# A table of offsets to the planner's order in a gated DeltaNet layer: heads' stages, out-projection operands and feed-forward groups

## The chip, the cores and the metric

The kernel runs on one core of one Trainium2 chip. The metric is device time in microseconds (us) of one execution; the median of three executions is compared. The core has a matrix engine (TensorE, "PE" in the profile, with its weight loads as "PEld"), a vector engine (VectorE, "DVE"), a scalar engine (ScalarE, "ACT"), GpSimd ("POOL") and a queue that issues DMAs (SyncE, "SP"). Each engine takes its own instructions strictly in the order in which the program holds them, and waits for the others through semaphores.

## The reference, cut to what matters

One layer (`DEPTH = 1`, so the gated DeltaNet mixer alone), 2048 tokens, width 1024: one input projection, eight heads of chunked linear attention and four heads of attention over a memory of 256 rows side by side, one output projection, a norm, a squared-ReLU feed-forward of width 4096, a norm.

```python
def gdn_mixer(x, mem_k, mem_v, w_in, conv_w, a_log, dt_bias, gate_norm_w, w_out):
    proj = x @ w_in                                   # q, k, v, z of 8 heads, gates a and b, queries to the memory
    qkv = silu(causal_depthwise_conv(proj[..., :3072], conv_w))
    q, k = l2_normalize(heads(q)), l2_normalize(heads(k))
    beta = sigmoid(b); g = -exp(a_log) * softplus(a + dt_bias)
    o = chunk_gated_delta_rule(q, k, v, g, beta)      # a triangular solve per chunk, then a recurrence over chunks
    o = rms_norm(o, gate_norm_w) * silu(heads(z))
    m = memory_attention(mq, mem_k, mem_v)
    return concatenate([o, m], axis=-1) @ w_out

x = layer_norm(ALPHA * x + gdn_mixer(x, ...), ln1_g, ln1_b)
x = layer_norm(ALPHA * x + square(relu(x @ w_ff1)) @ w_ff2, ln2_g, ln2_b)
```

## The kernel before

**Tiling and stages.** The 2048 tokens are four blocks of 512 (`b` = 0 to 3), taken two at a time (`s` = 0, 1). For each pair the program runs the mixer of block 2s, the mixer of block 2s+1, the output projection of both (`out_seven`), the first feed-forward product (`ff1`) and the second (`ff2`). The two blocks of a pair form one 2x2 block matrix product, done in seven products in place of eight, so operands such as A11, S2 or T3 are sums and differences of parts. Every large product is done three times over (`mm3`: high part by high, high by low, low by high), which needs each operand split into two parts: ACT casts the high part, DVE subtracts to get the low part (`split`, `split_in_place`). Weights go through a pool `whl` of four buffers; a weight tile is loaded by SP, cast by ACT and subtracted by DVE before PE may use all of it (its first two of three products need only the cast).

**A mixer** (`mixer(b, ...)`) has steps t = 0 to 9. In step t it records stage B (`gdn_b`, the recurrence of head t-2, and its delivery), stage A (`gdn_a`, decays, inverse of the 64x64 triangles and other preparations of head t-1), stage D (`dense`: the projections q, k, v of head t, whose matmuls write `aq`, `ak`, `av`, with convolution), stage Z (`gate`: the projection `az`), from t = 5 to 8 stage M (one head of attention over the memory: `amq`, `sps`, `pmT`, `pmo`), and in block 0 stage Y (`memory`: the memory's rows, keys `amk` and values `amv`, which are computed once). In block 1 two stages K and O prepare weights for later.

**The recurrence** of one head has four chunks, and each has the same chain across three engines: PE multiplies by the state (`pc<-state,ck`), DVE forms `R`, PE multiplies by the inverse (`pc<-R,Y`), ACT copies to `vt`, PE forms the state's update (`pc<-vt,kd`), DVE adds it to `state`, and the next chunk starts. `po` is the head's output, `pto` its transpose.

**What sets the order.** The functions do not issue anything: a `Recorder` keeps every operation in the order in which the code meets it. `issue()` (L291) then plans: it goes through a model of five engines with a cost for each operation (`cost`, L256) and a latency for each pair of engines, and whenever an engine comes free takes, of the operations that are ready on it, the one with the lowest `prio` (line 210). `prio` is the operation's number in the recording plus `shift`, a number set at a few places by hand. The operations are then issued, engine by engine, in the planned order, all from one line (L408), so that the profile tells groups apart by tile alone. Buffers are given out in the order in which the code first names them, whatever the `prio`: an operation that is moved ahead still waits for a buffer until those named before it have theirs.

**The output projection** (`out_seven`, with `part` inside) makes each operand (`operand`: X, from DRAM scratch `xo`) and its weights (`weights`: from `wos` scratch or `w_out`) when it is first needed. `ff1` starts with `second_half`, in which y is transposed (`pt<-ident,y`) and split into the operands `B`. While this goes on, `begin(p)` for p = 0 to 2 gives PE products that need none of it: `fA<-T,we` and `fB<-T,we`, with weights prepared in stage K. Then come 16 groups `rest(p)`.

Of the kernel before, what the change touches and what calls it, by code (L numbers as in the profile page):

```python
# [188 lines left out]

class Recorder:  # L190
    def __init__(self, nc, tc):
        self.nc, self.tc, self.ops, self.shift, self.gate = nc, tc, [], 0, None
# [13 lines left out]
    def add(self, eng, fn, name, args, kw):  # L206
# [3 lines left out]
        o.prio = o.i + self.shift  # L210
# [214 lines left out]
def hybrid_layer(  # L425
# [85 lines left out]
    nc = rec  # L511
    state = [rec.buf(cst, (P, P), F32, "state%d" % h, 1, "state") for h in range(H)]
# [763 lines left out]
    def second_half(ys, T0d, B, between):  # L1276
# [16 lines left out]
        for e2 in range(2):  # L1293
            c = slice(e2 * 2 * P, (e2 + 1) * 2 * P)
            for k in K2:
                if not e2:
# [25 lines left out]
    def ff1(s, ys, T0d, B):  # L1322
# [276 lines left out]
    def mixer(b, T, w0, G):  # L1599
        i = b % 2  # L1600
        r, A, z = {}, {}, {}
        for t in range(H + 2):
            if t >= 2:
                c = cat_tile()
                gdn_b(t - 2, A.pop(t - 2), G, z.pop(t - 2), c[0])
                deliver(i, t - 2, *c)
            if 1 <= t <= H:
                A[t - 1] = gdn_a(t - 1, r.pop(t - 1), G)
            if t < H:
                r[t] = dense(b, t, T, G, None if t else w0)  # L1610
            for n in Z_AT.get(t, ()):
                z[n] = gate(b, n, T)
            if t in MEM_AT:
# [3 lines left out]
                deliver(i, H + h, *c)  # L1617
            if b == 0 and t >= MEMORY:
                memory(t - MEMORY)
            if b == 1 and t in KEEP_FF:  # L1620
# [3 lines left out]
                rec.shift, rec.gate = 0, None  # L1624
            if b == 1 and 1 <= t <= 6:
# [11 lines left out]
    def out_seven(s, x1d, T0d):  # L1637
# [36 lines left out]
        def part(n, t, u, first, last):  # L1674
            xn, wn, bn, outs, on = OUT[n]
            if (n, u) not in xs:
                rec.gate = held.get(GATE.get(n))
                xs[n, u] = operand(n, xn, u)
                ws[n, u] = weights(wn, u)
                rec.gate = None  # L1680
# [35 lines left out]
        def first(t):  # L1716
            standardize(ys[t], x1d[t])
            if t % 2:
                keep_T(ys, T, T0d, t // 2)
# [126 lines left out]
```

## Time and profile before

| | us |
|---|---|
| median of three runs (2736.44 to 2738.46) | 2736.44 |
| the profiled execution's own time | 2735.04 |
| its span, from the first to the last instruction | 2733.3 |
| PE busy within the span | 2710.0 |
| DVE / ACT / POOL busy | 2109.6 / 1636.4 / 403.2 |
| mean granted TensorE clock | 0.999 |

The difference between the execution's time and its span, 1.7 us, lies outside the program's instructions. "Busy" counts the time in which at least one instruction of the engine is in flight. The stages follow each other on PE: both mixers of the first pair to about 655 us, output projection to 770, `ff1` to 1081, `ff2` to 1385, then the same for the second pair: mixers to 2005, projection to 2110, `ff1` to 2419, `ff2` to the end.

### The profile page before, as it was taken

The page shows a single profiled execution, that of the slowest core. Times are in us where ns is not written, and L with a number is a line of the kernel's source. Part 1 is how long each engine was busy: PE and PEld are TensorE (multiplying, and loading weights), DVE is VectorE, ACT ScalarE, POOL GpSimd, SP SyncE. Part 2 cuts the span into 40 slices and gives each one's busy share as a digit, 9 for nine tenths or more (in the row PEclk, how much of TensorE's full clock was granted, in tenths as well). Part 3 has the DMA queues.
Part 4 walks back from the last instruction along what each step waited for, and adds up shares of the span by engine and source line. Part 5 has one row for each costly group of instructions (what it writes and reads, how often), then busy time and mean ns, then how long its engine had stood idle before and what let it go on. Part 6 is the DMA issues. An engine that isn't in the chain of part 4 may idle for free.

```text
span 2733.3 us, 42460 instructions
## 1 busy us (share of the span) xinstructions
PE 2710.0 (99%) x13605; PEld 2267.3 (83%) x13605; DVE 2109.6 (77%) x5644; ACT 1636.4 (60%) x4106; POOL 403.2 (15%) x1030
## 2 busy tenths in 40 slices
PE   9999999999999999999999999999999999999998
PEld 7888888888888888888888888888888888888887
DVE  7899889998877777655778887888878666567575
ACT  7778767676475555334446766677756655553341
POOL 3233223321000000000033321232101000000000
PEclk9999999999999999999999999999999999999999
DMA  8666548876788888766754445444578644476673
GB/s 319 224 228 224 209 168 300 302 257 242 267 311 288 293 279 299 261 212 202 265 209 146 153 146 185 169 137 163 203 274 294 229 160 141 162 275 225 210 240 112
DMA packets 208543, 613.99 MB, mean 225 GB/s; under 512 B 23072, under 2 KB 32192, under 8 KB 188352
## 3 DMA queue, kind: packets, MB, share of 16 engines
q1 hardware_dynamic: 207888, 611.23, 64.2%
q8 instruction: 107, 1.75, 0.3%
q14 instruction: 116, 0.95, 0.1%
q10 hardware_dynamic: 432, 0.05, 0.0%
HBM read 436.54 MB, written 174.65 MB: 224 GB/s over the span
## 4 chain that ended last, share of the span: by engine, by line
PE 92%; DVE 4%; ACT 2%; issue 1%; DMA 1%; POOL 1%; SPq 0%; DVEq 0%; POOLq 0%; ACTq 0%
PE f2A L408 13%; PE fA L408 12%; PE ao L408 8%; PE f2C L408 6%; PE aq L408 6%; PE av L408 6%; PE fC L408 6%; PE az L408 6%; PE ak L408 6%; PE f2B L408 3%; PE pc L408 3%; PE amq L408 3%; PE fB L408 3%; PE po L408 2%; PE pkq L408 2%; PE pq L408 1%
## 5 line engine op out<-in xcount | busy, mean ns | idle before, releaser
L408 DVE TENSOR_TENSOR whl<-wraw,whl 128x512 fp32r<-128x512 f32 (+2 forms) x294 | 257.3, 884 | 111.2 <-ACT whl L408 108.6
L408 ACT CAST whl<-wraw 128x512 fp32r<-128x512 f32 (+2 forms) x294 | 226.6, 780 | 159.9 <-PE fC L408 54.7
L408 PE MATMUL fA<-B,whl 128*128 128x512 f32 x1152 | 276.9, 390 | 0.0
L408 PE MATMUL f2A<-whl,X 128*128 128x512 f32 x1152 | 262.1, 389 | 0.0
L408 ACT CAST X<-X 128x1024 fp32r<-128x1024 f32 x118 | 123.9, 1052 | 219.8 <-DMA X<-xsc 194.8
L408 PEld LDWEIGHTS fA<-B,whl 128*128 128x128 f32 x1152 | 216.1, 188 | 45.2 <-DVE B L408 0.2
L408 PEld LDWEIGHTS f2A<-whl,X 128*128 128x128 f32 x1152 | 216.3, 188 | 44.8
L408 DVE TENSOR_TENSOR X<-X,X 128x1024 fp32r<-128x1024 f32 x118 | 143.9, 1222 | 128.2 <-ACT X L408 128.0
L408 PE MATMUL aq<-T,whl 128*128 128x512 f32 x768 | 219.9, 411 | 5.6 <-ACT T L408 5.6
L408 PE MATMUL ak<-T,whl 128*128 128x512 f32 x768 | 215.3, 408 | 0.0
L408 PE MATMUL az<-T,whl 128*128 128x512 f32 x768 | 210.2, 405 | 0.0
L408 PE MATMUL av<-T,whl 128*128 128x512 f32 x768 | 208.2, 404 | 0.0
L408 PE MATMUL fC<-B,whl 128*128 128x512 f32 x768 | 185.6, 390 | 0.7 <-DVE B L408 0.7
L408 PE MATMUL f2C<-whl,X 128*128 128x512 f32 x768 | 174.7, 389 | 0.0
L408 PEld LDWEIGHTS fC<-B,whl 128*128 128x128 f32 x768 | 144.0, 188 | 31.4 <-DVE B L408 1.6
L408 PEld LDWEIGHTS f2C<-whl,X 128*128 128x128 f32 x768 | 144.2, 188 | 29.9
L408 PEld LDWEIGHTS aq<-T,whl 128*128 128x128 f32 x768 | 137.1, 192 | 27.7 <-ACT T L408 5.6
L408 PEld LDWEIGHTS av<-T,whl 128*128 128x128 f32 x768 | 138.4, 189 | 23.5
L408 PEld LDWEIGHTS ak<-T,whl 128*128 128x128 f32 x768 | 136.6, 189 | 22.3
L408 PEld LDWEIGHTS az<-T,whl 128*128 128x128 f32 x768 | 136.8, 189 | 22.0
L408 POOL TENSOR_SCALAR ve<-mv 128x1 f32<-128x1 f32 x34 | 16.8, 495 | 915.1 <-DVE mv L408 911.4
L408 PE MATMUL ao<-whl,X 128*128 128x512 f32 x528 | 139.8, 403 | 0.1
(294 smaller groups left out, 6272.4 us busy)
## 6 DMA issues: line engine op xcount, KB each, us to landing
whl<-wsc SPq DMA_DIRECT2D x108, 1024.0 KB, 5.0
wraw<-in_w_ff_dram SPq DMA_DIRECT2D x106, 512.0 KB, 4.6
X<-xsc SPq DMA_DIRECT2D x96, 512.0 KB, 3.9
wsc<-whl SPq DMA_DIRECT2D x36, 1024.0 KB, 6.1
whl<-tsc SPq DMA_DIRECT2D x64, 512.0 KB, 4.8
xsc<-hB SPq DMA_DIRECT2D x96, 256.0 KB, 3.1
xo<-cat SPq DMA_DIRECT2D x80, 256.0 KB, 3.9
wraw<-in_w_in_dram SPq DMA_DIRECT2D x35, 512.0 KB, 6.1
```

Source lines behind the costliest of these rows:

```text
L408: o.fn(*[res(a) for a in o.args], **{k: res(v) for k, v in o.kw.items()})
```

## The change

A table `PLACE` gives numbers to some stages. A new function `spot(*key)` looks its key up, and the number found (0 if there is none) is added to the `prio` of every operation recorded until the next call. So 82 places get an offset between -600 and +600: a negative one lets the operations of that stage go ahead of others that are ready, a positive one lets them stand back. No operation is added, removed or altered, and every engine has the same instructions before and after. Keys are (block, step, stage) in the mixers, (s, n, u, "X" or "W") for operand and weights of product n in the output projection, (s, p, "F") for feed-forward groups, (s, t, "n") for the standardization of a row tile after the output projection, and ("w",) for the three early groups.

```diff
+PLACE = {
+    ('w',): 445, (0, 0, 'F'): -65, (0, 1, 'Y'): 285, (0, 2, 'D'): -5, (0, 2, 'Y'): -225, (0, 2, 'n'): 600,
...
+    (1, 5, 0, 'X'): 10, (1, 5, 2, 'W'): -375, (1, 6, 0, 'W'): 15, (1, 6, 2, 'X'): -25,
+}
...
-        o.prio = o.i + self.shift
+        o.prio = o.i + self.shift + self.base
...
+    def spot(*key):
+        rec.base = PLACE.get(key, 0)
...
+        spot("w")
         between()
+        spot(None)
...
         for p in range(NP):
+            spot(s, p, "F")
             rest(p)
+            spot(None)
...
         for t in range(H + 2):
+            spot(b, t, "B")
             if t >= 2:
                 c = cat_tile()
                 gdn_b(t - 2, A.pop(t - 2), G, z.pop(t - 2), c[0])
                 deliver(i, t - 2, *c)
+            spot(b, t, "A")
             if 1 <= t <= H:
                 A[t - 1] = gdn_a(t - 1, r.pop(t - 1), G)
+            spot(b, t, "D")
             if t < H:
                 r[t] = dense(b, t, T, G, None if t else w0)
...
                 rec.gate = held.get(GATE.get(n))
+                spot(s, n, u, "X")
                 xs[n, u] = operand(n, xn, u)
+                spot(s, n, u, "W")
                 ws[n, u] = weights(wn, u)
+                spot(None)
```

The order on the engines, at three places that matter (rows of the built program, L408 before is L424 after).

**PE, block 0, first chunks of head 0's recurrence.** `pc`, `po` belong to the recurrence, `pp`, `pq` to the inverse of head 1, `ptk` to head 2's keys. Before:

```order
L408 MATMUL ptv<-ident,cv 128x128 x4
L408 MATMUL pp<-inv 112x32 x2
L408 MATMUL pc<-R,Y 128x128
L408 MATMUL ptk<-ident,ck 128x128 x4
L408 MATMUL pc<-vt,kd 128x128
L408 MATMUL po<-vt,at 128x128
L408 MATMUL pq<-Lq,inv 128x32 x2
L408 MATMUL pc<-state,ck 128x128
L408 MATMUL po<-state,qd 128x128
L408 MATMUL pp<-inv 128x32 x2
L408 MATMUL pc<-R,Y 128x128
L408 MATMUL pc<-vt,kd 128x128
```

After, from the same `pc<-vt,kd` on:

```order
L424 MATMUL pc<-vt,kd 128x128
L424 MATMUL po<-vt,at 128x128
L424 MATMUL aq<-T_187,whl 128x512
L424 MATMUL aq<-T_179,whl 128x512
L424 MATMUL aq<-T_206,whl 128x512
L424 MATMUL pc<-state,ck 128x128
L424 MATMUL po<-state,qd 128x128
L424 MATMUL pp<-inv 128x32 x2
L424 MATMUL aq<-T_213,whl 128x512
L424 MATMUL pc<-R,Y 128x128
L424 MATMUL aq<-T_206,whl 128x512 x2
L424 MATMUL aq<-T_213,whl 128x512
```

Matmuls of the next head's `aq`, which before had all been done by then, now stand between the links of the chain.

**PE, block 0, the keys of the memory.** `amk` are products for the keys, `az` belongs to the head before and `aq`, `ak`, `av` to the next. Before:

```order
L408 MATMUL az<-T_221,whl 128x512
L408 MATMUL amk<-mT,whl 128x256 x24
L408 MATMUL aq<-T_160,whl 128x512
L408 MATMUL aq<-T_165,whl 128x512
L408 MATMUL aq<-T_160,whl 128x512 x2
```

After:

```order
L424 MATMUL az<-T_221,whl 128x512
L424 MATMUL aq<-T_160,whl 128x512
L424 MATMUL amk<-mT,whl 128x256 x11
L424 MATMUL aq<-T_165,whl 128x512
L424 MATMUL ak<-T_160,whl 128x512
L424 MATMUL ak<-T_165,whl 128x512
L424 MATMUL av<-T_160,whl 128x512
L424 MATMUL av<-T_165,whl 128x512
L424 MATMUL amk<-mT,whl 128x256 x24
L424 MATMUL aq<-T_160,whl 128x512 x2
```

Three projections are begun with their first two matmuls, then a whole key product stands ahead of their rest.

**PE, first pair, the start of `ff1`.** `fB<-T,we` is the last of the early groups, `fC<-B,whl` the first product that needs the operands `B`. Before:

```order
L408 MATMUL fB<-T_10148,we 128x512
L408 MATMUL fB<-T_10135,we 128x512
L408 MATMUL fC<-B_10358,whl 128x512
L408 MATMUL fC<-B_10368,whl 128x512
L408 MATMUL fC<-B_10358,whl 128x512
L408 MATMUL fC<-B_10372,whl 128x512
```

After:

```order
L424 MATMUL fB<-T_10042,we 128x512
L424 MATMUL fC<-B_10358,whl 128x512
L424 MATMUL fC<-B_10368,whl 128x512
L424 MATMUL fC<-B_10358,whl 128x512
L424 MATMUL fC<-B_10372,whl 128x512
L424 MATMUL fC<-B_10378,whl 128x512
L424 MATMUL fC<-B_10372,whl 128x512
L424 MATMUL fB<-T_10135,we 128x512
L424 MATMUL fB<-T_10148,we 128x512
L424 MATMUL fB<-T_10135,we 128x512
L424 MATMUL fC<-B_10399,whl 128x512
```

All early groups stood ahead of the first `fC`; now part of the last one is spread among the first products that need `B`.

More of the change, by code (lines that the diff above doesn't have):

```diff
@@ L187 @@
                  "bufs", "turns", "prio", "quads", "cols", "late", "lhs")
+PLACE = {
[12 rows of a table added]
+}
 class Recorder:
     def __init__(self, nc, tc):
[L192 removed]
+        self.nc, self.tc, self.ops, self.shift, self.gate, self.base = nc, tc, [], 0, None, 0
         self.tags = {}
@@ L1295, in second_half @@
             for k in K2:
+                spot(e2, k, "H")
                 if not e2:
@@ L1606, in mixer @@
                 deliver(i, t - 2, *c)
+            spot(b, t, "A")
             if 1 <= t <= H:
                 A[t - 1] = gdn_a(t - 1, r.pop(t - 1), G)
+            spot(b, t, "D")
             if t < H:
                 r[t] = dense(b, t, T, G, None if t else w0)
+            spot(b, t, "Z")
             for n in Z_AT.get(t, ()):
                 z[n] = gate(b, n, T)
+            spot(b, t, "M")
             if t in MEM_AT:
@@ L1617, in mixer @@
                 deliver(i, H + h, *c)
+            spot(b, t, "Y")
             if b == 0 and t >= MEMORY:
                 memory(t - MEMORY)
+            spot(b, t, "K")
             if b == 1 and t in KEEP_FF:
@@ L1624, in mixer @@
                 rec.shift, rec.gate = 0, None
+            spot(b, t, "O")
             if b == 1 and 1 <= t <= 6:
@@ L1677, in part @@
                 rec.gate = held.get(GATE.get(n))
+                spot(s, n, u, "X")
                 xs[n, u] = operand(n, xn, u)
+                spot(s, n, u, "W")
                 ws[n, u] = weights(wn, u)
+                spot(None)
                 rec.gate = None
@@ L1716, in first @@
         def first(t):
+            spot(s, t, "n")
             standardize(ys[t], x1d[t])
+            spot(None)
             if t % 2:
```

10 rows, old and new, of the table PLACE are left out of this document.

## Prediction

> **What bounds the kernel now.** I read the page's first part, then the table of stages, then PE's timeline at the places where the table shows it idle, and last the order of both programs at those places. The page first:
>
> ```profile
> span 2733.3 us, 42460 instructions
> PE 2710.0 (99%) x13605; PEld 2267.3 (83%) x13605; DVE 2109.6 (77%) x5644; ACT 1636.4 (60%) x4106; POOL 403.2 (15%) x1030
> ```
>
> PE is in use all but 2733.3 - 2710.0 = 23.3 us, and the change gives it the same instructions. What an order can win is therefore a part of those 23.3 us, and of stops too short to show. The stages tell where they are (us, then PE, PEld, DVE, ACT and POOL busy, granted clock, DMA share, GB/s):
>
> ```profile
> 0.00:5.50 5.50, 0.00 (x0) 0.00 (x0) 2.65 (x10) 2.38 (x4) 4.86 (x25) 1.00 0.55 176
> 5.50:655.00 649.50, 643.48 (x3608) 542.89 (x3609) 580.07 (x2135) 483.17 (x1535) 190.79 (x472) 1.00 0.69 246
> 655.00:770.00 115.00, 113.90 (x551) 93.53 (x550) 94.09 (x171) 63.19 (x124) 9.83 (x23) 1.00 0.79 284
> 770.00:1081.00 311.00, 310.69 (x1386) 257.00 (x1386) 231.81 (x376) 186.41 (x322) 2.00 (x4) 1.00 0.84 290
> 1385.00:2005.00 620.00, 619.80 (x3498) 529.76 (x3497) 522.78 (x2022) 428.12 (x1459) 164.86 (x452) 1.00 0.50 174
> 2005.00:2110.00 105.00, 104.47 (x504) 86.38 (x503) 83.25 (x141) 56.54 (x102) 9.59 (x21) 1.00 0.80 281
> 2110.00:2419.00 309.00, 308.62 (x1377) 255.15 (x1376) 197.03 (x310) 182.94 (x319) 1.19 (x2) 1.00 0.53 181
> 2724.00:2733.30 9.30, 0.07 (x1) 0.00 (x0) 5.99 (x10) 0.00 (x0) 1.95 (x3) 0.73 0.30 113
> ```
>
> The first 5.5 us wait for the first loads and the last 9.2 us are the last norm on DVE: no key of the table reaches either. Left are 8.5 us: 6.0 in the first pair's mixers, 1.1 in its output projection, 0.3 at `ff1`, and in the second pair 0.2, 0.5 and 0.4. So the first pair's mixers are where something can be won, and the second pair's, with 0.2 us of shown idle in 620, where the same keys can mostly lose.
>
> A stop costs more than its shown idle time. Here are PE's rows in block 0 (start, time in flight, what, and the idle time before it with what ended it):
>
> ```profile
> 122.92 0.58 PE L408 MATMUL pp<-inv 128*112 128x32 f32 x4 [0.28 <-ACT inv L408]
> 123.85 0.49 PE L408 MATMUL pc<-R,Y 128*128 128x128 f32 x2 [0.35 <-DVE R L408]
> 125.08 0.49 PE L408 MATMUL pc<-vt,kd 128*128 128x128 f32 x2 [0.19 <-ACT vt L408]
> 125.41 0.39 PE L408 MATMUL po<-vt,at 128*128 128x128 f32 x2
> 125.63 0.53 PE L408 MATMUL pq<-Lq,inv 128*128 128x32 f32 x4
> 127.20 0.63 PE L408 MATMUL pp<-inv 128*128 128x32 f32 x4 [0.42 <-ACT inv L408]
> 128.51 0.49 PE L408 MATMUL pc<-vt,kd 128*128 128x128 f32 x2 [0.38 <-ACT vt L408]
> 128.84 0.39 PE L408 MATMUL po<-vt,at 128*128 128x128 f32 x2
> 129.66 0.49 PE L408 MATMUL pc<-state,ck 128*128 128x128 f32 x2 [0.43 <-DVE state L408]
> ```
>
> `pc<-vt,kd` at 125.08 is in flight for 0.49 us, but `po` starts 0.33 after it: 0.16 us of each group overlap with the next. Where PE has to stop, that overlap is lost too, so a stop costs its idle time and 0.16 us. [...]
>
> **The change part by part.** Nothing is added or removed, so each term is a stop that goes, shrinks or comes.
>
> *Head 0's recurrence, 122 to 130 us.* Six stops show 0.28 + 0.35 + 0.19 + 0.42 + 0.38 + 0.43 = 2.05 us, with 6 x 0.16 = 0.96 that is 3.0 us. The cause is that PE has nothing else: no wide matmul stands among these rows. In the changed order `aq` does, three of them between `pc<-vt,kd` with its `po` and `pc<-state,ck`. What one is worth comes from the chain's longest pure run:
>
> ```profile
> 1081.56 43.52 PE f2A L408 x192
> ```
>
> 43.52 / 192 = 0.227 us. From `pc<-vt,kd` (128.51) to `pc<-state,ck` (129.66) the chain took 1.15 us. In the new order `pc` and `po` take 0.33 + 0.22 (rows 128.51 and 128.84, and 125.41 to 125.63) and three `aq` 0.68, together 1.23: this link is covered, by little. The links through `R` and `vt` get one to five wide matmuls. I count -2.9; the bounds are -3.0 (all covered) and -1.5 (every second link still short, since cover of 1.23 against 1.15 fails if DVE or ACT take the step a little later).
>
> *Head 7's inverse and the start of `ff1`:*
>
> ```profile
> 632.76 0.63 PE L408 MATMUL pp<-inv 128*128 128x32 f32 x4 [0.43 <-ACT inv L408]
> 636.75 0.63 PE L408 MATMUL pq<-YP,inv 128*128 128x64 f32 x4 [0.51 <-ACT YP L408]
> 801.28 2.79 PE L408 MATMUL fC<-B,whl 128*128 128x512 f32 x11 [0.31 <-DVE B L408]
> ```
>
> The first two cost 0.43 + 0.51 + 2 x 0.16 = 1.26 us. In the changed order four more `ao` stand ahead of each of them, 4 x 0.227 = 0.91 against 0.59 and 0.67: gone, -1.2 (bounds -1.26 and 0). The third costs 0.47 us. Key "w" keeps early `fB` products back to fill it. But their weights lie in tiles that two later operands take over, so DVE may write the last parts of those only when the last `fB` is done:
>
> ```profile
> L408 DVE TENSOR_TENSOR whl<-wraw,whl 128x512 fp32r<-128x512 f32 x183 | 123.2, 688 | 60.2 <-ACT whl L408 59.0
> ```
>
> That is two such subtractions, 1.4 us, which before lay beside other work. I take -0.3, with bounds -0.47 and +1.4.
>
> *The memory's keys, block 0.* The changed order begins `aq`, `ak` and `av` with two matmuls each. Weights for `av` need the buffer that the first `amk` product frees; then ACT casts:
>
> ```profile
> 85.22 1.05 ACT L408 CAST whl<-wraw 128x1024 fp32r<-128x1024 f32 x1 [0.81 <-PE amk L408]
> 90.17 3.04 PE L408 MATMUL amk<-mT,whl 128*128 128x256 f32 x24
> 93.04 0.63 PE L408 MATMUL aq<-T,whl 128*128 128x512 f32 x2
> L408 DVE TENSOR_TENSOR whl<-wraw,whl 128x1024 fp32r<-128x1024 f32 x109 | 133.2, 1222 | 51.0 <-ACT whl L408 49.6 <-PE ptq L408 0.5
> ```
>
> From the start of the last `amk` about 0.2 + 1.05 us pass, and only one `aq` and two `ak`, 0.68 us, stand between: a stop of about 0.6 us that was not there. DVE's part for the rest (1.22) lies behind the second `amk` product (93.04 - 90.17 = 2.87). If DVE is late with it, three subtractions in a row are 3.7 against 2.87, and one more 1.2 is due. Value +0.6, bounds 0 and +2.
>
> *All other stops.* Of the 8.5 us, 2.05 + 0.94 + 0.31 are told above. About 0.9 belong to the first 12 us, where nothing moves. The other 4.3 lie at some 11 stops: PE's list of waits has 15 rows with 21 waits, from
>
> ```profile
> PE aq L408 <- ACT T L408: 5.6, 1, 5.6
> PE pp L408 <- ACT inv L408: 1.1, 3, 0.4
> ```
>
> to single ones of 0.2 us, and the start, the six, the two and the one told above are ten of them. With 0.16 each that is 4.3 + 1.8 = 6.1 us. Every one has the form of those above (a link of the recurrence, an inverse, a transpose, a weight just too late). In the order I find the cover of some of them longer and of some shorter. I take half of them as gone, -3.1. The bounds are -6 (all gone) and +6 (as many again: the second pair, nearly free of stops, has as many links as the first).
>
> Sum: -2.9 - 1.2 - 0.3 + 0.6 - 3.1 = -6.9 us, against the profiled 2735.04 that is 2728.1. The median stands 1.4 us above this execution, so the median comes to 2736.44 - 6.9 = 2729.5 us.
>
> **The rivals.** *DVE takes it back.* In the first pair's mixers DVE is busy 580.07 of 649.5 us, and in the worst stretch
>
> ```profile
> 450.00:500.00 50.00, 49.48 (x264) 40.68 (x263) 48.29 (x179) 35.05 (x112) 16.65 (x35) 1.00 0.89 322
> ```
>
> 48.29 of 50. PE gains 3 us at 130 us only to arrive earlier where DVE sets the pace; then only the gains behind 600 us remain, and -1.2 - 0.3 give 2735. Against it: over the whole stage DVE has 69 us to spare, and most stops wait for ACT. An offset that changes only the rank among operations that are ready may also do little: same result, and the order on PE speaks against it.
>
> *Slower: weights of the output projections come late.* Keys with "W" move SP's loads, the casts and the subtractions of whole operands by up to 600 places, and SP issues in order, so that a load behind one that waits for a buffer waits with it.
>
> ```profile
> whl<-wos SPq DMA_DIRECT2D x24, 512.0 KB, 5.2
> L408 ACT CAST whl<-whl 128x1024 fp32r<-128x1024 f32 x88 | 92.4, 1052 | 59.5 <-DMA whl<-tsc 30.7 <-DMA whl<-wos 15.6 <-DVE y L408 11.3
> L408 DVE TENSOR_TENSOR whl<-whl 128x1024 fp32r<-128x1024 f32 x88 | 107.6, 1223 | 13.9 <-ACT whl L408 13.2
> ```
>
> A reload takes 5.2 + 1.05 + 1.22 = 7.5 us, and the 24 matmuls of one part cover 5.4: a load that starts one part too late costs 2.1 us. Four such stops eat the 6.9 us, from there it is slower; six give +5.7, 2742. For it: at 2094 us the second pair already waits there, and in the changed order one of these reloads stands only 5.4 us of matmuls behind the one that frees its buffer. Against it: 0.5 us of idle in 105 today, and buffers still go in the old order. A stop that grows long would bring a second price:
>
> ```profile
> 5.57 7.16 PE L408 MATMUL aq<-T,whl 128*128 128x512 f32 x18 [5.57 <-ACT T L408]
> ```
>
> After the 5.57 us of waiting 18 matmuls took 7.16 us in place of 18 x 0.227 = 4.1, so 3 us more. [...]
>
> **How the numbers follow.** About 0.2%, 5.5 us, is what a measurement of this kernel can tell from no change: faster is below 2731, slower above 2741.9. The forecast has 0.57; its own range is 2722 to 2733 (other stops between -6 and 0, place one at -1.5), and 0.07 of it ends above 2731. DVE's case has 0.24, the slower one 0.19. That makes faster 0.50, same 0.07 + 0.24 = 0.31, slower 0.19. For the range, 2720 takes in all terms at their good bounds but the last few us (-3.0 - 1.3 - 0.5 - 6 = -10.8, and as much again for stops below 0.16 us that no view shows), 2742 the slower case with six stops; some 0.07 is left below and 0.12 above.
>
> **What would show it.** PE's idle time in the first pair's mixers falls from 6.0 to some 3 us, with no bracketed rows among head 0's `pc` and none at head 7's `pp` and `pq<-YP`; one stop of about 0.6 us before the first `av` after the first `amk`. In the second pair's mixers idle time stays under 1 us. The prediction is wrong if idle time at head 0's recurrence remains, if the second pair's stages lose several us, or if DVE's waits for PE shrink while PE's for DVE grow: then DVE sets the pace.

## The result, and the profile after

| us | before | after |
|---|---|---|
| median of 17 runs each (lowest to highest) | 2736.44 (2735.26 to 2739.12) | 2731.72 (2729.88 to 2733.23) |
| the profiled execution's own time | 2735.04 | 2731.02 |
| its span | 2733.3 | 2729.3 |

The ratio is 0.9982, with a 95% interval of 0.9975 to 0.9989: 4.7 us less by the medians, 4.0 us less by the spans of the two profiled executions. One number told above has to be put right: the table has 69 entries, not 82 (54 in the four mixers, 11 in the two output projections, 2 for feed-forward groups, 1 for the early groups and 1 for a standardization). The key ("w",) names no pair, so that its number stands at the start of `ff1` in both. The interval ends below 1, but by the prediction's own line (faster is below 2731) 2731.72 still counts as no change: it had given that 0.31, and a faster kernel 0.50.

The page of the changed kernel first, with the same two lines as above:

```profile
span 2729.3 us, 42448 instructions
PE 2707.3 (99%) x13605; PEld 2265.5 (83%) x13605; DVE 2106.6 (77%) x5644; ACT 1634.3 (60%) x4106; POOL 414.5 (15%) x1030
```

PE is still in flight for all but 22.0 us (before 23.3). Its busy time fell too, by 2.7 us, with the same 13605 matmuls. A part of this fits the overlap which a stop loses, as the prediction counted it: for the seven stops that PE's list of waits has fewer it would be 1.1 us (7 x 0.16). Another 0.7 us is in flight in PE's first row, 6.47 us where the prediction's row has 7.16:

```profile
5.55 6.47 PE L424 MATMUL aq<-T,whl 128*128 128x512 f32 x18 [5.55 <-ACT T L424]
```

PE takes the same matmuls in the same order up to far behind this place (the first difference is the 217th matmul, at 54 us), so that these 0.7 us are not owed to the table. For the remaining 0.9 us no row stands. The stages, in the table of the prediction (us, then PE, PEld, DVE, ACT and POOL busy, granted clock, DMA share, GB/s):

```profile
5.50:655.00 649.50, 644.60 (x3631) 545.21 (x3632) 585.64 (x2140) 485.84 (x1545) 193.45 (x472) 1.00 0.70 248
655.00:770.00 115.00, 114.69 (x557) 94.23 (x556) 92.08 (x171) 64.17 (x124) 13.32 (x26) 1.00 0.81 284
770.00:1081.00 311.00, 310.61 (x1381) 256.71 (x1380) 233.51 (x375) 184.97 (x317) 0.00 (x0) 1.00 0.83 291
1385.00:2005.00 620.00, 619.68 (x3500) 529.32 (x3500) 518.99 (x2031) 431.45 (x1467) 171.08 (x452) 1.00 0.49 176
2005.00:2110.00 105.00, 103.63 (x497) 85.19 (x496) 80.22 (x130) 54.60 (x95) 8.79 (x19) 1.00 0.77 273
450.00:500.00 50.00, 49.80 (x278) 41.81 (x277) 48.20 (x186) 37.94 (x129) 16.78 (x39) 1.00 0.92 327
```

PE's idle time fell in the first pair's mixers from 6.0 to 4.9 us and in its output projection from 1.1 to 0.3. It rose in the second pair's mixers from 0.2 to 0.3 and in its projection from 0.5 to 1.4. So idle time fell in the first half of the program and rose in the second. A fixed point between them shows what that is worth: the first `aq` matmul of the second pair. Its row in the list by line gives count, durations and the start of the first and the last one. Before, and then after:

```profile
L408 PE MATMUL aq<-T,whl x24: 388/389/390, 1390.9 to 1396.1; 128*128 128x512 f32 x24
```

```profile
L424 PE MATMUL aq<-T,whl x24: 389/389/389, 1385.5 to 1390.7; 128*128 128x512 f32 x24
```

The point came 5.4 us earlier. From there to the end of the span it was 1342.4 us before (2733.3 - 1390.9) and 1343.8 after: 1.4 us were given back.

The same can be done at other places. Where PE has done the same set of matmuls in both kernels, in whatever order, the starts of its next matmul can be compared, and what lies between two such places has its price:

| matmuls done | next start before | after | ahead by | in this stretch | what lies in it |
|---|---|---|---|---|---|
| 18 | 12.66 | 11.95 | 0.71 | -0.71 | the start, the same in both |
| 332 | 78.04 | 77.10 | 0.94 | -0.23 | other stops |
| 470 | 104.41 | 104.62 | -0.21 | +1.15 | the memory's keys |
| 675 | 139.58 | 136.70 | 2.88 | -3.09 | head 0's recurrence, and a new stop |
| 3467 | 628.98 | 626.25 | 2.73 | +0.15 | all other stops of the mixers |
| 3562 | 647.63 | 643.08 | 4.55 | -1.82 | head 7's inverse |
| 4235 | 785.10 | 779.52 | 5.58 | -1.03 | the output projection |
| 4355 | 812.10 | 806.74 | 5.36 | +0.22 | the start of `ff1` |
| 6912 | 1390.88 | 1385.50 | 5.38 | -0.02 | the rest of `ff1`, `ff2` |
| all | 2733.3 | 2729.3 | 4.0 | +1.4 | the second half |

Head 0's recurrence, and the two largest new stops, in PE's timeline of the changed kernel (start, time in flight, what, idle time before it and its releaser):

```profile
86.15 0.71 PE L424 MATMUL av<-T,whl 128*128 128x512 f32 x2 [0.96 <-DVE Bc L424]
...
117.63 0.73 PE L424 MATMUL aq<-T,whl 128*128 128x512 f32 x2 [0.97 <-DVE whl L424]
...
121.59 0.39 PE L424 MATMUL pc<-vt,kd 128*128 128x128 f32 x2
121.82 0.39 PE L424 MATMUL po<-vt,at 128*128 128x128 f32 x2
121.96 0.95 PE L424 MATMUL aq<-T,whl 128*128 128x512 f32 x3
122.74 0.38 PE L424 MATMUL pc<-state,ck 128*128 128x128 f32 x2
122.96 0.39 PE L424 MATMUL po<-state,qd 128*128 128x128 f32 x2
```

No row of the recurrence has a bracket any more. From `pc<-vt,kd` to `pc<-state,ck` PE again takes 1.15 us (122.74 - 121.59), as in the kernel before, but now three `aq` fill it. DVE had the state ready before PE asked for it:

```profile
122.02 0.35 DVE L424 SCALAR_TENSOR_TENSOR state<-state,el,pc 128x128 f32<-128x128 f32 x1 [0.29 <-PE pc L424]
```

It ended at 122.37. PE's weight load for `pc<-state,ck` began 0.14 us later, and the matmul itself at 122.74:

```profile
122.51 0.42 PEld L424 LDWEIGHTS pc<-state,ck 128*128 128x128 f32 x2
```

The other place of the prediction where a stop was feared is the second pair's output projection; PE's, ACT's and SP's rows there:

```profile
2091.25 0.72 PE L424 MATMUL ao<-whl,xh 128*128 128x512 f32 x2 [1.07 <-ACT whl L424]
```

```profile
2090.15 1.04 ACT L424 CAST whl<-whl 128x1024 fp32r<-128x1024 f32 x1 [0.78 <-DMA whl<-wos]
```

```profile
2084.90 0.32 SPq L424 DMA_DIRECT2D whl<-wos  x1
```

The reload was issued at 2084.90, ACT had its data at 2090.15, and PE stood 1.07 us for the cast.

### The profile page after: what moved, and what is told of

It reads as the page before. It is cut to its first block, busy times and chain, and to the rows that moved or that the text cites. A ratio compares the mean times of both kernels' runs of the same rounds, so it can differ in the third digit from the quotient of the medians.

```text
span 2729.3 us, 42448 instructions
## 1 busy us (share of the span) xinstructions
PE 2707.3 (99%) x13605; PEld 2265.5 (83%) x13605; DVE 2106.6 (77%) x5644; ACT 1634.3 (60%) x4106; POOL 414.5 (15%) x1030
## 4 chain that ended last, share of the span: by engine, by line
PE 92%; DVE 3%; ACT 3%; POOL 1%; issue 1%; DMA 1%; DVEq 0%; SPq 0%; POOLq 0%; ACTq 0%
PE f2A L424 13%; PE fA L424 13%; PE ao L424 8%; PE f2C L424 6%; PE fC L424 6%; PE av L424 6%; PE aq L424 6%; PE ak L424 6%; PE az L424 5%; PE f2B L424 3%; PE fB L424 3%; PE amq L424 3%; PE pc L424 3%; PE po L424 2%; PE pkq L424 2%; PE pq L424 1%
## 5 line engine op out<-in xcount | busy, mean ns | idle before, releaser
L424 DVE TENSOR_TENSOR whl<-wraw,whl 128x512 fp32r<-128x512 f32 (+2 forms) x294 | 257.0, 884 | 112.5 <-ACT whl L424 109.6
L424 ACT CAST whl<-wraw 128x512 fp32r<-128x512 f32 (+2 forms) x294 | 226.6, 780 | 158.6 <-PE fC L424 54.6
L424 PE MATMUL fA<-B,whl 128*128 128x512 f32 x1152 | 278.9, 389 | 0.0
L424 ACT CAST X<-X 128x1024 fp32r<-128x1024 f32 x118 | 123.9, 1052 | 231.2 <-DMA X<-xsc 203.2
L424 PE MATMUL f2A<-whl,X 128*128 128x512 f32 x1152 | 262.1, 389 | 0.0
L424 PEld LDWEIGHTS fA<-B,whl 128*128 128x128 f32 x1152 | 216.1, 188 | 45.3 <-DVE B L424 0.3
L424 PEld LDWEIGHTS f2A<-whl,X 128*128 128x128 f32 x1152 | 216.3, 188 | 44.8
L424 DVE TENSOR_TENSOR X<-X,X 128x1024 fp32r<-128x1024 f32 x118 | 144.0, 1221 | 128.8 <-ACT X L424 128.8
L424 PE MATMUL aq<-T,whl 128*128 128x512 f32 x768 | 216.5, 409 | 6.5 <-ACT T L424 5.5
L424 PE MATMUL av<-T,whl 128*128 128x512 f32 x768 | 221.9, 405 | 1.0 <-DVE Bc L424 1.0
L424 PE MATMUL az<-T,whl 128*128 128x512 f32 x768 | 222.8, 404 | 0.0
L424 PE MATMUL ak<-T,whl 128*128 128x512 f32 x768 | 210.8, 405 | 0.0
L424 PE MATMUL fC<-B,whl 128*128 128x512 f32 x768 | 186.8, 389 | 0.4 <-DVE B L424 0.4
L424 PE MATMUL f2C<-whl,X 128*128 128x512 f32 x768 | 174.7, 389 | 0.0
L424 PEld LDWEIGHTS fC<-B,whl 128*128 128x128 f32 x768 | 144.0, 188 | 31.0 <-DVE B L424 0.8
L424 PEld LDWEIGHTS f2C<-whl,X 128*128 128x128 f32 x768 | 144.2, 188 | 29.9
L424 PEld LDWEIGHTS aq<-T,whl 128*128 128x128 f32 x768 | 136.8, 191 | 28.7 <-ACT T L424 5.5
L424 PEld LDWEIGHTS av<-T,whl 128*128 128x128 f32 x768 | 137.8, 189 | 24.2 <-ACT mst L424 1.4
L424 PEld LDWEIGHTS ak<-T,whl 128*128 128x128 f32 x768 | 137.3, 189 | 23.5
L424 PEld LDWEIGHTS az<-T,whl 128*128 128x128 f32 x768 | 137.9, 189 | 22.3
L424 POOL TENSOR_SCALAR ve<-mv 128x1 f32<-128x1 f32 x34 | 16.8, 493 | 918.3 <-DVE mv L424 917.8
L424 PE MATMUL ao<-whl,X 128*128 128x512 f32 x528 | 139.9, 404 | 0.3 <-DVE whl L424 0.3
```

The lines of the kernel that those rows point to most:

```text
L424: o.fn(*[res(a) for a in o.args], **{k: res(v) for k, v in o.kw.items()})
```

## The experiments

Every experiment is the changed kernel with a part of its table (the eleventh with all signs turned), so that the work is the same in each. Differences are between medians, against the kernel before run on the same chip in the same series (27 to 33 runs of it; 11 of each experiment, 4 of the eleventh).

| entries kept | median | before | difference | ratio, 95% interval |
|---|---|---|---|---|
| all 69 | 2731.72 | 2736.44 | -4.7 | 0.9975 to 0.9989 |
| 1: 12 of block 0 | 2738.73 | 2736.87 | +1.9 | 0.9998 to 1.0016 |
| 2: all but those | 2735.19 | 2736.87 | -1.7 | 0.9986 to 1.0003 |
| 3: one alone | 2732.66 | 2736.87 | -4.2 | 0.9975 to 0.9993 |
| 4: all but 6 of the second projection | 2737.38 | 2736.87 | +0.5 | 0.9993 to 1.001 |
| 5: first half, 32 | 2730.39 | 2736.53 | -6.1 | 0.9968 to 0.9986 |
| 6: second half, 37 | 2738.07 | 2736.53 | +1.5 | 0.9998 to 1.0015 |
| 7: the one of 3 and the 57 of 2 | 2738.90 | 2736.53 | +2.4 | 0.9999 to 1.0017 |
| 8: 12 of block 0, 5 of the first projection | 2738.59 | 2736.53 | +2.1 | 1.0001 to 1.0018 |
| 9: 12 of block 0, 12 of block 1 | 2732.45 | 2736.79 | -4.3 | 0.9973 to 0.9991 |
| 10: first half less (0,6,'D') | 2733.18 | 2736.79 | -3.6 | 0.9977 to 0.9995 |
| 11: all, signs turned | 2777.73 | 2736.79 | +40.9 | 1.0131 to 1.0163 |
| 12: all but 30 of the second mixers | 2731.31 | 2736.79 | -5.5 | 0.9969 to 0.9986 |

An interval is about 2.4 us wide to each side. In 1, 2, 4, 6 and 7 it takes in 1, so that the sign of these differences is not shown.

**1. Block 0's mixer alone.**

```diff
 PLACE = {
-    ('w',): 445, (0, 0, 'F'): -65, (0, 1, 'Y'): 285, ...
+    (0, 1, 'Y'): 285, (0, 2, 'D'): -5, (0, 2, 'Y'): -225, (0, 5, 'A'): 175, (0, 5, 'M'): -20, (0, 6, 'A'): -145,
+    (0, 6, 'B'): -200, (0, 6, 'D'): 90, (0, 6, 'Z'): 325, (0, 7, 'B'): -600, (0, 7, 'D'): -170, (0, 8, 'B'): -430,
 }
```

> Only the 12 keys of block 0's mixer are kept. Theory (the gain is single stops of TensorE that go, place by place): head 0's recurrence at 122 to 130 us is covered as in the whole table, worth 3.0 us, and the two new stops of 1.1 us each (before av, at 86 us; before aq, at 118 us) come with it; nothing else is touched on purpose, so 1 to 3 us under before, 2733.5 to 2735.5. Rival (VectorE takes it back in the first pair's mixers): within 1 us of before, with new waits for DVE between 130 and 650 us. Rival (the gain is spread over all stages): under 1 us.

Measured: 2738.73, a miss by 3 us: no gain is left. The recurrence was covered as expected, but the first output projection, in which no entry was kept, got new stops. PE there:

```profile
689.56 0.71 PE L414 MATMUL ao<-whl,xh 128*128 128x512 f32 x2
...
693.44 0.49 PE L414 MATMUL pc<-vt,kd 128*128 128x128 f32 x2 [0.41 <-ACT vt L414]
...
695.99 2.78 PE L414 MATMUL ao<-whl,xh 128*128 128x512 f32 x7 [1.84 <-ACT whl L414]
```

ACT in the same microseconds:

```profile
693.12 0.27 ACT L414 COPY vt<-pc 128x128 f32<-128x128 f32 x1 [2.96 <-PE pc L414]
693.28 1.05 ACT L414 CAST whl<-whl 128x1024 fp32r<-128x1024 f32 x1
...
694.90 1.03 ACT L414 CAST whl<-whl 128x1024 fp32r<-128x1024 f32 x1
```

Both casts of weights stand behind a copy of head 7's recurrence in ACT's queue. The copy waited 2.96 us for PE, and the queue with it; 3.6 us after PE had begun the `xh` products the last copy was just starting. A second stop, 1.85 us for DVE's part of a weight, follows at 722; what delayed that one is not traced. Compared as in the table of stretches, PE is 3.3 us ahead of the kernel before at 673 us and 2.7 us behind it at 769. So an order changed in block 0 moved the plan 600 us later, to a place where ACT's order decides.

**2. Everything but block 0's mixer.**

```diff
 PLACE = {
-    (0, 1, 'Y'): 285, (0, 2, 'D'): -5, (0, 2, 'Y'): -225, ... (0, 8, 'B'): -430,
 }
```

> The table without the 12 keys of block 0's mixer (57 of 69 left). Theory: the six stops of head 0's recurrence are back (3.0 us), the two new stops of 1.1 us are gone, and the gains behind 600 us (head 7's inverse, output projection, together about 2 us) less the reload at 2091 us (1.2 us) stay: 0 to 2 us under before, 2734.5 to 2736.5. Rival (gain spread over all stages): about 4 us under before, as with the whole table.

Measured: 2735.19, as expected. Head 0's recurrence has its stops again; those of head 7's inverse are gone without block 0's entries. (The third experiment shows that one entry of block 0 alone removes them too.)

**3. One entry.**

```diff
 PLACE = {
-    ('w',): 445, (0, 0, 'F'): -65, ...
+    (0, 2, 'Y'): -225,
 }
```

> One key alone, (0, 2, Y): -225, the memory's keys of step 2 ahead by 225. By the order its recurrence of head 0 is covered (three or more wide matmuls between the links), and av is not begun behind the first key product, so its 1.1 us stop should not come. Theory: 2.5 to 4 us under before, 2732.5 to 2734, more than the twelve keys of block 0 together. Rival (VectorE sets the pace, the cover only moves the stop): the same 1 us stop before aq at 118 us and others of its kind, within 1.5 us of before. Rival (many keys are needed): within 1 us.

Measured: 2732.66. The size is as expected: this one number, which lets the memory's work of step 2 go ahead, brings what the whole table brings within the intervals. The place is not quite: the recurrence got one long stop for the six short ones, and the clock fell after it. PE's row, and the granted clock in the stretches behind it (stretch, length, PE busy, clock, DMA share, GB/s):

```profile
124.28 0.69 PE L413 MATMUL pc<-R,Y 128*128 128x128 f32 x2 [1.27 <-DVE R L413]
```

```profile
124.00:125.00 1.00, 0.72 (x4) 0.72 1.01 426
125.00:127.00 2.00, 2.00 (x11) 0.50 0.99 416
127.00:128.00 1.00, 1.00 (x6) 0.58 0.72 291
```

Much of its gain lies elsewhere. Between 495 and 754 us PE has no stop, so that both of head 7's inverse and the one of 0.57 us at 697 are gone, with no entry near them. Against the kernel before PE gains 1.6 us between 104 and 157 us, loses 0.3 from there to 626, and gains 1.9 between 626 and 769.

**4. Without the six entries of the second output projection.**

```diff
 PLACE = {
-    (1, 0, 0, 'W'): -355, (1, 1, 2, 'W'): -600, (1, 5, 0, 'X'): 10, (1, 5, 2, 'W'): -375,
-    (1, 6, 0, 'W'): 15, (1, 6, 2, 'X'): -25,
 }
```

> The whole table without the six keys of the second pair's output projection. Theory: the stop of 1.24 us before ao at 2091 us (weights reloaded only 5.4 us of matmuls behind the buffer's release) and that of 0.47 at 2053 go, and the stop of 0.7 us that before had there comes back: 0.5 to 1.5 us under the whole table, 2730.2 to 2731.2. Rival (those keys win elsewhere in that stage or in ff1 behind it): 0 to 1 us over the whole table.

Measured: 2737.38, a miss by 6 us. The 1.07 us stop at 2091 went, as expected. But at the change from the mixer to the projection PE now stood for

```profile
2002.86 0.63 PE L423 MATMUL pq<-YP,inv 128*128 128x64 f32 x4 [1.48 <-DVE YP L423]
...
2056.92 15.68 PE L423 MATMUL ao<-whl,X 128*128 128x512 f32 x68 [1.24 <-DVE whl L423]
```

and 0.45 and 0.56 us between them. Its span is 3.9 us longer than that of the whole table, its median 5.7. The profiled execution is the fastest of the eleven; nine of them, but not this one, have a mean clock of 0.998. Lost clock may be what the other runs add, but no trace shows it. So a projection's entries can only be judged together with the mixers' ahead of them.

**5 and 6. The two halves.** The fifth leaves out the entries of the second pair, as below; the sixth keeps these alone. The entry ("w",), which acts in both pairs, is in the fifth.

```diff
 PLACE = {
-    (1, 6, 'F'): -45, (2, 1, 'Z'): -60, ... (3, 8, 'Z'): 115, (1, 0, 0, 'W'): -355, ... (1, 6, 2, 'X'): -25,
 }
```

> Only the entries up to the first output projection and the start of the first feed-forward stand in the table (12 of the first block's mixer, 12 of the second's, 5 of the first output projection, the weights of the gate, the memory entry n and the first feed-forward entry: 32 of 69). Before: 2736.9. Theory A (the gain lies in the first pair of blocks, in the recurrence at 122 to 130 us, in head 7's inverse and in the first output projection; the second pair's 37 entries win nothing of their own): 2731 to 2733, with the second output projection like that of the kernel before (idle of PE 0.5 us between 2005 and 2110, no stop over 0.8 us there). Rival B (an order upstream shifts the plan downstream, so half a table spoils the later stages as the 63 entries did by 5 us): over 2735, with a stop of over 1 us between 1990 and 2110. Rival C (the gain is spread over the whole program): about 2734.5.

> The other half alone: the third and fourth blocks' mixers, the second output projection and the second feed-forward entry (37 of 69). Before: 2736.9. Theory A: no gain, 2736.5 to 2738.5; the stop behind the late weights near 2091 to 2095 us comes back with about 1 us, the recurrence of head 0 keeps its six stops. Rival C (spread over the program): 2734 to 2735. If parts add, this run's difference and that of the first half sum to the whole table's -4.7 us within 1.5 us; if they do not, the plan couples the two halves.

Measured: 2730.39 and 2738.07, differences of -6.1 and +1.5, together -4.6 against -4.7 for the whole. The halves add, as far as intervals of 2.4 us can tell. The sixth has the stop of 1.1 us behind late weights, as expected; no new stop came into the second half of the fifth. Its second output projection is that of the kernel before, and its point between the halves with its span (2729.1) gives the second half 1342.5 us, as in the kernel before (1342.4):

```profile
2005.00:2110.00 105.00, 104.47 (x505) 1.00 0.80 281
```

```profile
L418 PE MATMUL aq<-T,whl x24: 389/389/389, 1386.6 to 1391.8; 128*128 128x512 f32 x24
```

**7. The one entry with the 57.**

```diff
 PLACE = {
-    (0, 1, 'Y'): 285, (0, 2, 'D'): -5, (0, 5, 'A'): 175, ... (0, 8, 'B'): -430,
 }
```

> The one entry (0,2,'Y') of the first block's mixer, with all 57 entries that are not of that mixer. Before: 2736.9. If the gains add: the one entry alone gave -4.2 us and the 57 gave -1.7, so 2731 (2730 to 2732), the best of all. Rival B (coupling): the first output projection gets stops of over 1 us behind weights that are converted late, as with the first block's entries alone, and the time is 2734 or more. A stop of 1.27 us behind R at 124 us is expected in any case, after which the granted clock may show 0.5 for about 3 us (1 to 1.5 us of the profile's own time, not always there).

Measured: 2738.90. What gave -4.2 and -1.7 apart gives +2.4 together: inside one half, gains do not add. The largest new stop is at the place of the first experiment, but for the cast of an operand (`xh`) and not of a weight:

```profile
695.28 0.73 PE L422 MATMUL ao<-whl,xh 128*128 128x512 f32 x2 [2.10 <-ACT xh L422]
```

**8 and 9. What repairs the projection?** Block 0's entries with the first projection's, then with block 1's mixer's.

```diff
 PLACE = {   # the eighth
     (0, 1, 'Y'): 285, ... (0, 8, 'B'): -430,
+    (0, 0, 2, 'X'): 150, (0, 1, 0, 'X'): 140, (0, 5, 1, 'X'): 225, (0, 5, 2, 'X'): 155, (0, 6, 0, 'W'): -150,
 }
 PLACE = {   # the ninth
     (0, 1, 'Y'): 285, ... (0, 8, 'B'): -430,
+    (1, 2, 'D'): 335, (1, 3, 'A'): 150, (1, 3, 'B'): 300, ... (1, 6, 'B'): -550, (1, 6, 'D'): -165, (1, 7, 'Z'): -60,
 }
```

> The 12 entries of the first block's mixer, which alone gave +1.9 us with 5.9 us of new stops in the first output projection, and the 5 entries of that projection. Theory D (the projection's entries repair what the mixer's entries spoil there): the stops of 1.84 and 1.85 us near 696 and 722 us are gone, 2732 to 2733.5. Rival E (the repair needs the second block's entries too, since the stopped conversion stands behind head 7's recurrence in ScalarE's queue): the stops stay, 2737 to 2739.

> The 12 entries of the first block's mixer and the 12 of the second's, without those of the output projection, the gate's weights and the feed-forward. Before: 2736.5. Theory E (what the first block's entries spoil near 696 us, a conversion of weights that stands behind copies of head 7's recurrence in ScalarE's queue, is put right by the second block's entries, which move that recurrence): no stop over 1 us between 690 and 725 us, 2731 to 2733. If neither is true and all 17 of block 0 and the projection plus the rest are needed: 2737 or more, the stops of 1.8 us still there.

Measured: 2738.59 with the stops of 1.83 and 1.85 us still there, and 2732.45 without them. Block 1's entries do it: in the ninth's profile head 7's recurrence has ended before the `xh` products begin. ACT's and PE's rows of the ninth:

```profile
688.71 0.27 ACT L416 COPY vt<-pc 128x128 f32<-128x128 f32 x1 [3.15 <-PE pc L416]
...
691.50 1.04 ACT L416 CAST whl<-whl 128x1024 fp32r<-128x1024 f32 x1
```

```profile
690.53 0.62 PE L416 MATMUL ao<-whl,xh 128*128 128x512 f32 x2
```

The last copy now starts 1.8 us before PE's first `xh` product; in the first experiment it started 3.6 us after it.

**10. The first half without one entry.**

```diff
 PLACE = {
-    (0, 6, 'D'): 90,
 }
```

> The first half's 32 entries (2730.4 us) without (0,6,'D') : 90. In the order, no instruction of TensorE between 640 and 740 us then stands nearer behind the one that feeds it than that feed takes in the trace of before (with the 32, a remaining shortfall of 0.4 us). Theory A (the gain is the sum of single stops): the same or up to 0.7 us faster than the first half, 2729.5 to 2730.5. Rival B (any entry taken out shifts the plan downstream, as with 63 of 69): over 2733.

Measured: 2733.18, at the edge of what rival B gives. In its profile PE has no idle time at all from 655 to 770 us, which is what taking the entry out was for. But the two stops of head 7's inverse are back, 0.36 and 0.67 us at 631 and 635 us, and stops of 0.57, 0.36 and 0.55 us stand at 452, 526 and 796 us. Its interval overlaps that of the first half, so that the loss is not certain.

**11. All signs turned.**

```diff
 PLACE = {
-    ('w',): 445, (0, 0, 'F'): -65, ...
+    ('w',): -445, (0, 0, 'F'): 65, ...
 }
```

> All 69 entries with their signs turned: as large a shuffle, in the other direction. Before: 2736.5. Rival F (the order before is poor, and any shuffle of this size helps): under 2735. Theory A (each entry pays by one named stop; a shuffle that is not chosen adds stops): head 0's recurrence keeps its six stops, new stops in the output projections and before the first feed-forward, 2741 to 2750.

Measured: 2777.73, +41 us, so it is not the case that any shuffle of this size helps. More than half of it is lost where `ff1` begins and the early groups are used up (11.6 us in the first pair and 11.3 in the second, by the comparison of stretches), at stops such as

```profile
800.96 1.12 PE L424 MATMUL pt<-ident,y 128*128 128x128 f32 x4 [2.02 <-ACT b L424]
```

and in the output projections (2.44 us for DVE's `whl` in each).

**12. Without the second pair's mixers' entries.**

```diff
 PLACE = {
-    (2, 1, 'Z'): -60, (2, 3, 'A'): 340, ... (3, 7, 'Z'): 315, (3, 8, 'Z'): 115,
 }
```

> The whole table without the 30 entries of the third and fourth blocks' mixers; the six of the second output projection stay. Before: 2736.5, whole table 2731.7, first half 2730.4. Theory A (the second pair's mixers had nothing to win; the 0.85 us that their entries cost go): 2730.5 to 2732, with the 1.07 us stop near 2091 us still there, since it comes from the projection's own entries. Rival B (the projection's entries were fitted to those of the mixers): a new stop over 1 us at 1990 to 2060 us, 2733 or more.

Measured: 2731.31, as the first theory had it, with a stop of 1.00 us at 2091.82. The point between the halves and its span (2729.9) give the second half 1342.7 us, against 1343.8 with those 30 entries:

```profile
L419 PE MATMUL aq<-T,whl x24: 389/389/389, 1387.2 to 1392.5; 128*128 128x512 f32 x24
```

The fifth and the twelfth are faster than the whole table by 0.8 to 1.4 us against their own runs of the kernel before. The intervals overlap, so neither is shown to beat it.

## Why the prediction came out as it did

Sign and range were right: 2729.5 was predicted and 2731.72 measured. The sum of -6.9 us was too good by 2.2 in the median, and by 2.9 in the profiled executions. That it came so near is in part luck, for its terms were further off, in both directions. In the table of stretches (profiled executions):

- **Head 0's recurrence** (-2.9): cause and place right, all six stops gone. But the stretch is 3.09 us shorter although it holds a new stop of 1.1 us (below), so the recurrence gave 4.2, beyond the good bound of -3.0. Mis-sized by 1.3. All eight profiles that keep block 0's twelve entries show these 3.1 us. A stop cost more than its idle time and 0.16 us: from `pc<-vt,kd` to the next `po` it is 0.33 us in the rows of before and 0.23 in those of the changed kernel (121.59 to 121.82). The rest of the difference is not traced. The link of 1.15 us is covered, by 0.14 us at the weight load, nearly as little as the 0.08 that was worked out.
- **Head 7's inverse** (-1.2): both stops gone, and 1.8 us gained; again beyond the good bound (-1.26).
- **The start of `ff1`** (-0.3): mis-sized; a stop of the same kind is still there (0.39 us at 797, before 0.31), and the stretch is 0.2 us longer. The bad bound, +1.4, was not reached.
- **The memory's keys** (+0.6): the stop before the first `av` came, but 0.96 us long, and the stretch is 1.15 longer. Mis-sized by 0.5. The row ends with DVE's `Bc`, and not with the cast that the prediction timed; why PE waits for that is not traced.
- **A term that was missing**: the 0.97 us stop before `aq` at 117.63, 1.1 us with the overlap. It stands just ahead of the place whose stops were removed: PE takes `aq` weights there while DVE's part of them, 1.2 us in that form, has just been done. The cover given to the recurrence was not free.
- **All other stops** (-3.1): -0.2 and +0.15 in the first pair's mixers, -1.0 in its output projection and +1.4 in the second half, together +0.3. This is the step that failed. "Half of them go" is not what happened: outside the two named places the stops of the first pair's mixers show 2.5 us of idle time before, and 2.4 in the changed kernel without the two new ones told above. They were exchanged for others. The second pair, with 0.2 us of idle in 620, was named as the place where entries can mostly lose, and then got no term of its own.
- **The start**: 0.7 us of the 4.0 between the two profiled executions are chance. PE begins with the same matmuls in all fourteen profiles, and the first 18 take from 6.3 to 8.0 us.

The sum is -4.2 - 1.8 + 0.2 + 1.15 + 1.1 + 0.3 - 0.7 = -4.0. So the two named gains were 1.9 us better than forecast and the unnamed ones 3.4 us worse. The lower end of the stated range of the forecast, 2722, is also further down than its bounds go (2736.4 - 10.8 = 2725.6).

One profile of each kernel carries only so far. The fourth, fifth and twelfth experiment have the order of the changed kernel on PE throughout the first half; from the 18th matmul to the fixed point the four take 1372.9 to 1374.3 us, and the kernel before 1378.2. So the first half is 3.9 to 5.3 us shorter without the start. The second half takes 1342.1 to 1343.4 us in the five profiles that have PE's order of before there (before, 1, 3, 8, 9), and 1343.7 to 1343.8 in the three with that of the changed kernel (changed, 2, 7). So the entries of the second pair cost about 1.1 us; leaving out the 30 of its mixers gave 1342.7, in one profile.

Of the signs that the prediction named, most are there: no bracketed rows at head 0's `pc` and at head 7's `pp` and `pq<-YP`, one new stop before `av`, under 1 us of idle time in the second pair's mixers. One is not: idle time in the first pair's mixers fell to 4.9 us and not to some 3, because of the new stops (0.97, 0.96 and 0.84 us).

How the waits of PE changed can be read in its list (engine, tile, releaser: total, times, longest), here of the changed kernel; it went from 15 rows with 21 waits to 12 with 14:

```profile
PE aq L424 <- ACT T L424: 5.5, 1, 5.5
PE ao L424 <- ACT whl L424: 1.1, 1, 1.1
PE aq L424 <- DVE whl L424: 1.0, 1, 1.0
PE av L424 <- DVE Bc L424: 1.0, 1, 1.0
...
PE pp L424 <- DVE inv L424: 0.2, 1, 0.2
```

Fewer and longer: before, none but the first was over 0.6 us; now one is 0.8 and three are about 1 us, and these are what an engineer would attack next.

**The rivals.** *DVE takes it back* did not happen: between 450 and 500 us DVE is busy 48.20 us (before 48.29), and PE's idle time there fell from 0.52 to 0.20. Its mechanism shows at single places: by PE's lists its waits for DVE grew from 3.7 to 4.2 us, while those for ACT, without the start, fell from 4.0 to 2.3, and two of the three long new stops end with DVE. *Late weights in the output projections* was right in place, and stronger than its one stop in the changed kernel shows. That one stop, at 2091, cost 1.2 us where 2.1 was estimated: PE waited only for the cast (5.25 us of load and 1.04 of cast behind 2084.90), not for DVE's part as well. In five of the twelve experiments (1, 4, 7, 8, 11) stops of 1.2 to 2.4 us stand at these places, for weights in 1, 4, 8 and 11 and for an operand's cast in 7. In 1, 7 and 8 they cost the whole gain; in 4 a stop of 1.48 us for a mixer's inverse comes to them, and in 11 the greater part is lost at `ff1`. At 2091 a load came late, as described (ACT waited 0.78 us for it). In the experiments, where it was followed, the mechanism was another: not SP's queue, but ACT's, in which the casts stand behind the recurrence's copies (the first stop of 1, repaired in 9). *The second price of a stop that grows long* had been read from one row: 3 us more behind a wait of 5.57 us, with the granted clock written as 1.00. The runs showed a second price behind short stops too: in the sixth experiment the granted clock fell to 0.50 behind stops of at most 0.42 us, and this drop cost 2.75 us (last section).

The same numbers explain why an entry has no price of its own. A stop that goes is a gain at its place, but the plan behind it shifts, and at the two changes from mixer to projection it can lose 4 to 7 us (PE's lead over the kernel before, between 673 and 769 us in 1, 7 and 8, and between 1979 and 2113 in 4). The halves added (5 and 6), and the traces show that their plans are separate: PE's order in the second half is the same in the kernel before, 1, 3, 8 and 9, with five different sets of entries in the first half, and the same in the changed kernel, 2 and 7. Entries inside a half did not add (1, 2, 4, 7). `ff1` and `ff2` lie between the halves, long chains that wait for almost nothing (in the first pair before, PE is idle for 0.3 us in 311 and 0.0 in 304); that these are what separates them was not tested by itself.

## What to carry to other kernels

Count a table of offsets as a list of single stops: those that go and those that come. Do not book stops that you have not followed as half gone: here they were exchanged for others. Give every stage a term, and give a stage with nothing to win only a cost. Read the result at places where the same work has been done in both kernels; that gave prices which the idle times alone did not. Test such a table by halves that are cut at a stage without waits, not by leaving out single entries, whose effect is felt hundreds of microseconds later. Where one stage hands over to the next, look in the helper engine's own queue for what stands ahead of the work that the next stage needs first.

## What the runs showed of the hardware

The granted clock fell to 0.50 after quite short stops too, for 3.4 us or for two or three times that. The recurrence of head 0 in the sixth experiment has the order of the kernel before, from 119 us on, and stops of at most 0.42 us. Its clock by stretches (length, PE busy, clock, DMA share, GB/s):

```profile
119.00:129.00 10.00, 8.52 (x53) 1.00 0.90 364
129.00:130.00 1.00, 0.84 (x4) 0.74 0.00 0
130.00:136.00 6.00, 5.82 (x26) 0.50 0.00 0
136.00:137.00 1.00, 1.00 (x6) 0.85 0.00 0
```

Half the clock over a share (1 - 0.74) / 0.5 = 0.52 us, 6 us and 0.30 us makes 6.8 us. In the third experiment the same sum is 0.56 + 2 + 0.84 = 3.4 us. All twelve drops within the profiles (without the one at the end of each, where PE has run out of work) last, summed like this from stretches of 1 us, 3.4 (eight), 6.8 (two) or 10.2 us (two). So each lasted one, two or three times 3.4 us.

What it costs can be read from one pair of rows, `ptv` before and behind the place. Before:

```profile
121.98 0.66 PE L408 MATMUL ptv<-ident,cv 128*128 128x128 f32 x4
...
133.85 0.60 PE L408 MATMUL ptv<-ident,cv 128*128 128x128 f32 x4
```

The sixth experiment:

```profile
122.61 0.66 PE L419 MATMUL ptv<-ident,cv 128*128 128x128 f32 x4
...
137.23 0.60 PE L419 MATMUL ptv<-ident,cv 128*128 128x128 f32 x4
```

14.62 us against 11.87: 2.75 us for 6.8 us at a clock of 0.50, where by an estimate (6.8 x 0.5) 3.4 would be lost if PE had not had to wait in any of it. The drop does not come every time: the same instructions showed none in the profile before (1.00 from 119 to 137 us). Of the four profiles that keep the stops of that recurrence three show a drop there (2, 6, 11), of the eight without stops in the recurrence none, and both with one stop of 1.27 or 1.28 us (3, 7). The runs without a profile have only their mean clock, which is listed to three digits. Of 93 runs of the kernel before, 49 had 0.999, 34 had 0.998 and 10 had 0.997, the medians of these groups being 2736.1 to 2736.6, 2737.1 to 2737.5 and 2738.2 to 2739.5 in the three series. Of the changed kernel all 17 had 0.999. In the three series the median of all runs of the kernel before lies 0.3 to 0.4 us above that of its runs with 0.999. By this estimate 0.3 to 0.4 us of what the change wins in the median is clock that is no longer lost. The recurrence is not the only place for it: 1, 4 and 8 have no stops there, yet seven, nine and eight of their eleven runs are below 0.999, and in the profiles of 1 and 8 the drops follow the stops of 1.8 us at the output projection. Which stops a drop follows, the runs do not tell: stops of 1.48 and 1.07 us passed without a drop in the profiles of 4 and of the changed kernel.
